# Casting FFN weights in DRAM ahead of their first use, paced by the FFN stages

## The chip, the cores and the metric

The kernel runs on all 8 cores of one Trainium2 chip, two dies of four cores. Each core computes two of the 16 sequences; the cores exchange nothing. The metric is the device time of one execution in microseconds (us): that of the slowest core.

Many executions fall into a slower state, whatever the kernel: all cores of one die, sometimes of both, show a lower granted clock and the time is several per cent longer. Such executions are called slow and are not compared. Fast ones of one kernel lie within about one per cent of each other.

## The reference, cut to what matters

```python
D_MODEL, BATCH, SEQ, D_FF = 1024, 16, 2048, 2816
def reference(x, ...):
    for l in range(2):
        x = ln(alpha*x + 0.5*swiglu(x, ffn_w_gate_up[l,0], ffn_w_down[l,0]))   # FFN 0, FFN 2
        y = hgrn2(x, ...) if l == 0 else forgetting_attention(x, k, v, c, ...)
        x = ln(alpha*x + y)
        x = ln(alpha*x + 0.5*swiglu(x, ffn_w_gate_up[l,1], ffn_w_down[l,1]))   # FFN 1, FFN 3
        if l == 0: k, v, c = shared_kv(x, ...)
    return x
```

The four FFNs carry most of the arithmetic. One has 22 gate/up tiles (1 MB each in float32, 0.5 MB in bf16) and 5.8 MB of down weights in bf16. All inputs are float32; the kernel multiplies in bf16.

## The kernel before

A core walks over 8 blocks of 512 tokens. The work is recorded as a sequence of tokens; `p0` is FFN 0 of the first two blocks together, `a`, `c`, `d`, `e` are FFN 0, 1, 2, 3 of one block, `h` the recurrence, `k` the keys and values, `x` the attention. Recurrence and attention are a second thread, woven into the FFN stages by a list scheduler. That scheduler works at build time, with a cost model, and fixes the order of instructions on each engine.

```python
head = "p0 i2 h0 a2 h1 h2 c0 k0 d0 x0 c1 k1 d1 x1 c2 k2 d2 e0 x2 i3 a3 e1 h3 i4 a4"
```

Weights come through one helper. At the first use GpSimd's DMA queue (POOL) casts float32 in DRAM to bf16 in SBUF, and the plain queue of SyncE (SP) writes the bf16 tile back to a scratch in DRAM; every later use is a plain load from that scratch.

```python
def wload(self, th, key, dst, bufs, chan, scr, src, nb):
    R = self.R
    wb = self.wsb.get(key)
    if wb is None:                                     # first use
        wb = self.wsb[key] = Buf()
        R.dma("pool", [(dst, src)], reads=..., writes=bufs, chan=chan, nbytes=nb)
        R.dma("sp", [(scr, dst)], reads=bufs, writes=[wb], chan=self.wch.next(), nbytes=nb)
    else:
        R.dma("sp", [(dst, scr)], reads=[wb], writes=bufs, chan=chan, nbytes=nb)

def ffn(self, blocks, f):                              # cut
    for half in range(2):
        for jj in range(HJ):                           # 2 x 11 steps
            j = half * HJ + jj
            w = self.wg.next()                         # a ring of 5 tiles
            self.wload(0, ("gu", f, j), w.t[:], ...)
            if jj in (1, 3, 5): ...                    # a group of down weights into wd
            ...                                        # 16 matmuls a block, ACT, DVE -> hT[:, jj]
        ...                                            # down projection, layer norm in the second half
```

The softmax here doesn't subtract the row's maximum and nothing guards it: scores larger than these inputs give would overflow.

## Time and profile before

| | before |
|---|---|
| executions | 5817.2, 5830.1, 5835.0, 5844.3 us; two slow ones 6309.9 and 6460.6 us |
| core 3 of the profile | 5825.7 us, PE busy 94% |

The profile of before caught a slow execution: die 1 ran at a clock of 0.925. So I read core 3, on the undisturbed die. PE is the matrix engine. An FFN stage is taken to end with the last matmul that reads the down weights `wd` (each block has 176 of them, so the count gives the stage). The stages of core 3, in order p0, a2, c0, d0, c1, d1, c2, d2, e0, by the table of stretches; the columns are the stretch, its length, the busy time of PE, weight loads, DVE, ACT and POOL with their instructions, the granted PE clock, the DMA share (mean busy share of 16 DMA engines) and GB/s:

```profile
core 3: us, PE busy (x) PEld busy (x) DVE busy (x) ACT busy (x) POOL busy (x), PEclk, DMA share, GB/s
0.00:331.00 331.00, 279.14 (x1178) 120.44 (x1179) 125.00 (x215) 39.73 (x61) 26.51 (x54) 0.88 0.79 175
331.00:544.00 213.00, 191.59 (x1015) 87.57 (x1013) 138.02 (x297) 108.26 (x235) 19.88 (x25) 0.97 0.73 191
544.00:801.00 257.00, 215.73 (x1111) 98.38 (x1110) 154.96 (x320) 116.64 (x247) 30.93 (x43) 0.92 0.88 214
801.00:1133.00 332.00, 279.06 (x1440) 129.19 (x1438) 201.47 (x398) 136.96 (x271) 33.88 (x53) 0.91 0.90 214
1133.00:1311.00 178.00, 167.27 (x1039) 83.78 (x1038) 92.64 (x158) 58.59 (x114) 5.50 (x10) 0.98 0.67 215
1311.00:1474.00 163.00, 151.64 (x699) 67.16 (x697) 69.15 (x110) 25.98 (x38) 3.23 (x4) 0.97 0.60 182
1474.00:1648.00 174.00, 168.41 (x1044) 84.69 (x1043) 92.96 (x158) 58.82 (x114) 4.39 (x8) 0.98 0.59 196
1648.00:1809.00 161.00, 148.02 (x694) 65.73 (x692) 68.54 (x109) 25.87 (x38) 6.69 (x10) 0.99 0.68 202
1809.00:2046.00 237.00, 194.92 (x1356) 99.16 (x1354) 91.43 (x158) 91.56 (x177) 17.34 (x31) 0.91 0.87 211
```

Length minus PE busy is PE's idle time: 42 us in e0, 41 and 53 us in c0 and d0, 6 to 13 us in each of c1, d1, c2 and d2. The stages with first uses (p0, c0, d0, e0) have a DMA share near 0.8 to 0.9, the others about 0.6 to 0.7.

Names in the views: `wg` is the ring of gate/up tiles, `wd` the down weights, `wgu_s` and `wdn_s` their bf16 scratch in DRAM, `lw` a weight tile of the recurrence or attention, `rD` and `rL` residual rows, `xbD` and `xbL` layer norm's output in bf16, `mv` layer norm's statistics, `hT` the FFN's hidden values, `pb` a PSUM bank.

What e0's PE waited for (waiter, awaited: us in total, times, longest):

```profile
PE pb L1096 <- DMA fka_2_72<-ka_d: 30.7, 3, 22.9
PE pb L1096 <- DMA fka_2_73<-ka_d: 5.4, 1, 5.4
PE pb L686 <- ACT xbD L677: 4.3, 2, 2.7
...
PE pb L639 <- DMA wg_7<-w_gu: 0.4, 1, 0.4
```

The awaited load is not a weight: `fka` holds the attention's keys. It is late because SP's queue is full of e0's write-backs and other traffic, as the issue timeline of SP shows (start, time that the issue took, what):

```profile
1825.83 0.34 SPq L242 DMA_DIRECT2D rD_17<-xr_d  x1
1826.21 3.21 SPq L242 DMA_DIRECT2D rL_21<-xr_d  x1
1832.27 12.05 SPq L242 DMA_DIRECT2D wdn_s<-wd  x2
1844.36 15.00 SPq L242 DMA_DIRECT2D fka_2_72<-ka_d  x1
```

An issue takes about 0.3 us when the queue has room, and 15 us for `fka` here.

### The profile page before, as it was taken

The numbers are of one execution on the slowest core, as the hardware profiler recorded it, in microseconds if no ns is written. First come the engines' busy times: TensorE is split into PE (matmuls) and PEld (weight loads), VectorE is DVE, ScalarE is ACT, GpSimd is POOL, SyncE is SP. The second block draws the span as 40 slices with busy tenths as digits, with TensorE's granted clock in tenths as the row PEclk, the third lists the DMA queues.
The fourth block names the chain that finished last, engine by engine and source line by source line (L and its number), as shares of the span: only waits on it lengthen the run. The fifth ranks groups of instructions, "written<-read, shape, count | busy, mean of one in ns | idle before, by whom it ended". The sixth has DMA issues, their size and how long they took to land.

```text
span 6089.9 us, 77661 instructions; the slowest of 8 cores (5798.2 to 6089.9 us)
## 1 busy us (share of the span) xinstructions
PE 5759.3 (95%) x31296; PEld 2685.6 (44%) x31296; DVE 3064.1 (50%) x5516; ACT 2134.0 (35%) x4154; POOL 272.7 (4%) x410
## 2 busy tenths in 40 slices
PE   6987979999998999999999999999999999999999
PEld 2443434444444444444544454444544444534543
DVE  2466656554542567674557535674245543333344
ACT  0153535322214153442325262442513415514510
POOL 0001111000000000000000000000000000000000
PEclk9998989999998999999999999999888788878887
DMA  9678897775678656566564656555354454454344
GB/s 213 155 201 217 194 240 183 222 222 184 199 185 219 211 188 204 178 196 196 180 211 147 200 182 205 177 189 197 109 192 151 148 169 137 135 181 146 109 157 137
DMA packets 383494, 1106.28 MB, mean 182 GB/s; under 512 B 66784, under 2 KB 80800, under 8 KB 370592
## 3 DMA queue, kind: packets, MB, share of 16 engines
q1 hardware_dynamic: 353840, 1004.80, 50.1%
q0 software_dynamic: 29296, 96.51, 10.1%
q8 instruction: 248, 4.06, 0.3%
q14 instruction: 110, 0.90, 0.1%
HBM read 989.54 MB, written 208.14 MB: 197 GB/s over the span
## 4 chain that ended last, share of the span: by engine, by line
PE 84%; DMA 8%; DVE 3%; ACT 2%; issue 2%; POOL 0%; SPq 0%; POOLq 0%; DVEq 0%
PE pb L639 73%; PE pb L1096 4%; PE pb L1112 2%; DMA wg_6<-w_gu 1%; PE pb L686 1%; PE pb L949 1%; DMA fka_2_72<-ka_d 1%; DMA lw_38<-hqf_s 1%; DMA wg_9<-wgu_s 1%; DMA wg_7<-w_gu 1%; DMA ka_d<-hT 1%; PE pb L928 1%; DMA wgu_s<-wg_7 1%; DMA xr_d<-rL_21 1%; PE pb L945 0%
## 5 line engine op out<-in xcount | busy, mean ns | idle before, releaser
L639 PE MATMUL pb<-wd,hT 128*128 128x512 bf16 x5456 | 1319.6, 396 | 6.3 <-DVE sg_14 L723 3.3
L639 PEld LDWEIGHTS pb<-wd,hT 128*128 128x128 bf16 x5456 | 539.3, 101 | 656.1 <-issue 219.8
L720 ACT ACTIVATE sg_13<-pb 128x512 f32<-128x512 f32 x352 | 209.9, 596 | 977.7 <-PE pb L639 976.2
L720 ACT ACTIVATE sg_14<-pb 128x512 f32<-128x512 f32 x352 | 210.0, 596 | 973.5 <-PE pb L639 971.2
L723 DVE SCALAR_TENSOR_TENSOR sg_14<-sg_14,pb 128x512 f32<-128x512 f32 x352 | 241.5, 686 | 569.4 <-ACT sg_14 L720 568.7
L723 DVE SCALAR_TENSOR_TENSOR sg_13<-sg_13,pb 128x512 f32<-128x512 f32 x352 | 241.5, 686 | 510.3 <-ACT sg_13 L720 509.5
L726 DVE SCALAR_TENSOR_TENSOR hT<-sg_14,pb 128x512 bf16<-128x512 f32 x352 | 241.2, 685 | 201.2 <-PE pb L639 186.9
L726 DVE SCALAR_TENSOR_TENSOR hT<-sg_13,pb 128x512 bf16<-128x512 f32 x330 | 225.9, 685 | 190.1 <-PE pb L639 179.2
L639 PE MATMUL pb<-xT_3,wg_6 128*128 128x512 bf16 x880 | 223.0, 403 | 44.3 <-DMA wg_6<-w_gu 42.7
L639 PE MATMUL pb<-xT_4,wg_10 128*128 128x512 bf16 x912 | 232.9, 405 | 7.7 <-DVE hT L980 5.3
L639 PE MATMUL pb<-xT_3,wg_10 128*128 128x512 bf16 x880 | 218.9, 399 | 18.7 <-DMA wg_10<-w_gu 8.0
L639 PE MATMUL pb<-xT_3,wg_8 128*128 128x512 bf16 x896 | 224.4, 399 | 10.7 <-DMA wg_8<-w_gu 8.7
L639 PE MATMUL pb<-xT_4,wg_6 128*128 128x512 bf16 x912 | 229.7, 403 | 0.0
L639 PE MATMUL pb<-xT_3,wg_7 128*128 128x512 bf16 x880 | 221.4, 401 | 8.3 <-DMA wg_7<-w_gu 6.0
L639 PE MATMUL pb<-xT_4,wg_9 128*128 128x512 bf16 x848 | 216.2, 405 | 7.2 <-ACT hT L977 1.8
L639 PE MATMUL pb<-xT_4,wg_8 128*128 128x512 bf16 x880 | 220.2, 400 | 2.7 <-DVE hT L980 1.0
L639 PE MATMUL pb<-xT_4,wg_7 128*128 128x512 bf16 x864 | 216.3, 400 | 1.3 <-ACT hT L977 0.9
L639 PE MATMUL pb<-xT_3,wg_9 128*128 128x512 bf16 x880 | 214.4, 394 | 0.3 <-DMA wg_9<-wgu_s 0.3
L639 PE MATMUL pb<-xT_5,wg_9 128*128 128x512 bf16 x592 | 144.7, 390 | 12.9 <-DMA wg_9<-wgu_s 9.0
L639 PEld LDWEIGHTS pb<-xT_3,wg_6 128*128 128x128 bf16 x880 | 87.8, 102 | 154.3 <-issue 66.2
L639 PE MATMUL pb<-xT_5,wg_7 128*128 128x512 bf16 x608 | 147.6, 387 | 3.5 <-DVE sg_14 L723 1.9
L1105 ACT ACTIVATE fPT_2_76<-pb 128x512 bf16<-128x512 f32 (+1 forms) x216 | 122.3, 566 | 73.6 <-PE pb L1096 40.2
(507 smaller groups left out, 9471.2 us busy)
## 6 DMA issues: line engine op xcount, KB each, us to landing
wd<-wdn_s SPq DMA_DIRECT2D x108, 1024.0 KB, 7.4
wg_9<-wgu_s SPq DMA_DIRECT2D x120, 512.0 KB, 4.4
wg_10<-wgu_s SPq DMA_DIRECT2D x120, 512.0 KB, 4.6
wg_8<-wgu_s SPq DMA_DIRECT2D x119, 512.0 KB, 4.6
wg_7<-wgu_s SPq DMA_DIRECT2D x118, 512.0 KB, 4.5
wg_6<-wgu_s SPq DMA_DIRECT2D x117, 512.0 KB, 4.6
wd<-wdn_s SPq DMA_DIRECT2D x54, 768.0 KB, 9.6
wd<-w_dn POOLq DMA_DIRECT2D x16, 1024.0 KB, 16.9
```

The costliest lines, as they stand in the source:

```text
L639: ins = e.matmul(out, lhsT=pairs[i][0], rhs=pairs[i][1], start=(start and i == 0), stop=(stop and i == n - 1))
L686: ins = e.transpose(qv[:, k, :], xb.t[:, k * 128:(k + 1) * 128], self.ident.t[:])
L720: R.op("act", lambda e, sg=sg, pg=pg: e.activation(out=sg.t[:], in_=pg.t[:], func=AF.Tanh, scale=0.5), reads=[pg.b], writes=[sg.b], cost=c ...
L723: R.op("dve", lambda e, sg=sg, pg=pg: e.scalar_tensor_tensor(out=sg.t[:], in0=sg.t[:], scalar=1.0, in1=pg.t[:], op0=ALU.add, op1=ALU.mult) ...
L726: R.op("dve", lambda e, sg=sg, pu=pu, jj=jj, hT=hT: e.scalar_tensor_tensor(out=hT[:, jj, :], in0=sg.t[:], scalar=0.25, in1=pu.t[:], op0=AL ...
L928: ins = e.matmul(Uv[:, x, :], lhsT=bt.t[:, t, :], rhs=V.t[:, t, hv], start=True, stop=True)
L949: R.op("pe", lambda e, t=t, cc=cc, c=c, pov=pov, A=A, sp=sp: e.matmul(pov[cc * 64:(cc + 1) * 64, t, :], lhsT=A.t[:, c * 64:(c + 1) * 64], ...
L1096: first = ins = e.matmul(ps.t[:, c0:512], lhsT=ka.t[:, i * 128:(i + 1) * 128], rhs=qa.t[:, h4, c0:512], start=True, stop=(i < 4 * b))
L1105: R.op("act", lambda e, ps=ps, pt=pt, c0=c0: e.activation(out=pt.t[:, c0:512], in_=ps.t[:, c0:512], func=AF.Exp), reads=[ps.b], writes=[pt ...
L1112: ins = e.matmul(accv[:, t, 0:65], lhsT=pt.t[:, t * 128:(t + 1) * 128], rhs=Vt.t[:, i, vo:vo + 65], start=(i == 0 and t == 0), stop=(i == ...
```

## The change

The intent: some weights of FFN 1, 2 and 3 are cast from DRAM to the bf16 scratch in DRAM in an earlier FFN stage, one tile or down group at a time, each released by a step of that stage. Their first use is then a plain load, and the write-back falls away. FFN 1: 17 of 22 gate/up tiles, in the second half of p0 and in a2. FFN 2: 8 tiles, in c0. FFN 3: all 22 tiles and the 6 down groups, in c1, d1, c2, d2. That is 53 casts.

```diff
+    def precast(self, key, gate):
+        if key[0] == "gu":
+            scr, src, nb = self.wgu_s[key[1:]], self.wgu_f[key[1:]], 1 << 19
+        else:
+            ...                                   # the rows of one down group
+        wb = self.wsb[key] = Buf()
+        self.R.dma("pool", [(scr, src)], reads=[gate], writes=[wb], chan=self.cch, nbytes=nb * 1.3)
@@ record
+        gu = lambda f, a, b: [("gu", f, j) for j in range(a, b)]
+        dn = lambda f: [("dn", f, half, g) for half in range(2) for g in range(3)]
+        pre = {"p0": [None] * 11 + gu(1, 0, 11), "a2": gu(1, 11, 17), "c0": gu(2, 0, 8),
+               "c1": gu(3, 0, 7), "d1": gu(3, 7, 14), "c2": gu(3, 14, 22), "d2": dn(3)}
@@ ffn
+        npq = list(self.pq)
+                due = len(npq) * (j + 1) // NJ - len(npq) * j // NJ
+                step = [Buf()] if due else []
-                        reads=[sg.b, pu.b], writes=[hTb[jj]] + ([self.gate] if ...),
+                        reads=[sg.b, pu.b], writes=[hTb[jj]] + step + ([self.gate] if ...),
+                for _ in range(due):
+                    key = self.pq.pop(0)
+                    if key:
+                        self.precast(key, step[0])
```

`chan=self.cch` makes each precast wait for the one before.

## The prediction

> **What bounds the kernel now.** I read core 3, the slowest of the undisturbed die (5825.7 us). By its page the matrix engine (PE) is busy 94% and the chain of waits is 83% PE, 8% DMA: PE-bound, except early. The table of 100 us windows:
> - 0 to 500 us (FFN 0, two blocks at once): 72 us idle, 51 of it in the first 100 us, on first weight loads.
> - 500 to 1150 us (first uses of FFN 1 and 2): about 95 us idle, DMA share 0.77 to 1.01. The PE timeline shows waits for `lw` loads (9.9, 8.6, 14.8 us) and for stores and loads behind `hT`, `xb`, `rD`.
> - 1800 to 2000 us (first use of FFN 3): 42 us idle, DMA share 0.97 and 0.78; waits of 22.9, 6.4, 5.4 us for `fka<-ka_d`. The issue timeline shows single SP issues taking 12 and 15 us: the queue is backed up.
> - 1150 to 1800 us: DMA share 0.5 to 0.7, PE 88 to 100% busy, with room. After 2050 us PE idles about 2%.
>
> **What the change does.** From the packet records, a cast packet leaving 4096 B takes 0.41 us, a plain one 0.20 us. A gate/up tile (128 rows, 16 engines) costs about 3.3 us of all 16 engines to cast, 1.6 us to write back. A whole first-use FFN needs about 160 us (estimate), against 52 us read from scratch. The change drops the write-back but adds a reload, so the total hardly moves; work moves in time. (The Trainium skill, "DMA: Bandwidth & Descriptors", section "Issuing engines are not separate DMA queues", says all issuers share 16 engines, so I count one budget; section "SWDGE vs HWDGE vs iDMA" says a casting DMA must come from GpSimd. The trace agrees: all casts stand on POOL's queue.) Estimates, DMA time:
> - FFN 0, second half: +36 us (11 casts); the next FFN stage +20 us (6).
> - First use of FFN 1: -29 us; of FFN 2: -26 us.
> - c1, d1, c2, d2: +23, +23, +26, +39 us, into a share of 0.5 to 0.7.
> - First use of FFN 3: -110 us.
>
> **Critical path.** At FFN 3 nearly all DMA idle should go: 35 us. In 500 to 1150 us the load falls by a tenth and SP no longer stands behind write-backs of 17 and 8 tiles: 25 to 35 us of 95. Against it, FFN 0's second half (share 0.85) gets more; each precast waits for the one before, on the in-order POOL queue, ahead of FFN 0's own casts (landing in 10 to 24 us): 10 to 20 us lost. The casts in 1150 to 1800 us cost at most 5 us. Steady state is unchanged. Net 40 to 65 us.
>
> **Predicted time:** fast executions lie at 5817 to 5844 us. I expect 5778 us, 8 in 10 between 5715 and 5845. Chances: faster by over 2% 0.13, within 2% 0.82, slower by over 2% 0.05.
>
> **What would show it.** Right: in 1800 to 2000 us PE idle under 15 us, DMA share under 0.75, no long `fka` wait; 53 fewer casts into `wg` and `wd`, as many fewer write-backs; DMA share up by 0.2 in 1200 to 1700 us without new idle; in 500 to 1150 us idle of 60 to 70 us. Wrong: new waits in 200 to 500 us on `wg<-w_gu` or `wg<-wgu_s`.
>
> **What would make it wrong.** DRAM-to-DRAM casts much dearer than casts into SBUF; POOL stuck behind precasts, so that layer norm's `pow` is late; casts that finish after their first use; a shifted order of the list scheduler in the steady state.

## More of the kernel before

The costs of casts at their first use, from the list of DMA issues (destination, source, queue, count, KB, median us from issue to landing):

```profile
wg_6<-w_gu POOLq DMA_DIRECT2D x20, 512.0 KB, 9.3
wgu_s<-wg_6 SPq DMA_DIRECT2D x20, 512.0 KB, 10.9
```

## The result, and the profile after

The kernel after took 5847.29 us in the median of its 10 timed executions, 4 of them slow; the fast ones lie between 5840.7 and 5847.7 us. The ratio to before is 1.0026, 95% interval 1.0010 to 1.0042. Ratios here are the mean time of one kernel's fast executions over that of the other's in the same rounds, so not quite the ratio of the medians. The change is worth nothing, or costs a quarter of a per cent.

The profile of after is a fast one. Core 3 again, by stages:

```profile
core 3: us, PE busy (x) PEld busy (x) DVE busy (x) ACT busy (x) POOL busy (x), PEclk, DMA share, GB/s
0.00:308.00 308.00, 243.56 (x1096) 108.26 (x1097) 110.57 (x192) 31.99 (x50) 28.35 (x58) 0.94 0.90 190
308.00:536.00 228.00, 200.37 (x1029) 90.36 (x1027) 139.93 (x293) 107.87 (x230) 21.57 (x31) 0.95 0.82 200
536.00:802.00 266.00, 231.93 (x1228) 107.91 (x1228) 173.26 (x358) 127.92 (x265) 31.38 (x43) 0.95 0.83 200
802.00:1115.00 313.00, 265.53 (x1376) 122.44 (x1377) 191.69 (x381) 132.61 (x267) 30.36 (x42) 0.92 0.82 205
1115.00:1318.00 203.00, 177.05 (x1051) 87.44 (x1049) 95.66 (x162) 59.57 (x115) 9.84 (x18) 0.92 0.81 222
1318.00:1482.00 164.00, 151.59 (x700) 67.15 (x699) 69.33 (x111) 25.98 (x38) 6.90 (x11) 0.97 0.73 207
1482.00:1669.00 187.00, 170.22 (x1042) 84.59 (x1040) 92.00 (x157) 58.84 (x114) 8.72 (x16) 0.97 0.72 202
1669.00:1836.00 167.00, 152.90 (x698) 67.46 (x697) 69.52 (x110) 25.87 (x38) 6.92 (x10) 0.96 0.82 212
1836.00:2031.00 195.00, 188.97 (x1350) 97.46 (x1348) 92.67 (x160) 90.43 (x177) 4.99 (x9) 0.98 0.61 188
```

e0 (last row) is 42 us shorter, with 6 us idle; its DMA share fell from 0.87 to 0.61. But a2, c0, c1 and c2 (rows 2, 3, 5 and 7) are longer by 15, 9, 25 and 13 us; d0 is 19 us shorter, d2 6 us longer. The first row must be read with care. In before, core 3 ran at a clock of 0.81 for 144 us of p0, and the cores beside it did not:

```profile
100.00:239.00 139.00, 137.75 (x639) 62.29 (x638) 50.76 (x74) 17.32 (x29) 10.23 (x18) 1.00 0.83 166
...
100.00:239.00 139.00, 138.06 (x527) 57.04 (x526) 41.26 (x60) 13.12 (x22) 9.79 (x18) 0.81 0.75 152
```

(cores 1 and 3 of before, the same stretch.) The Trainium skill, "TensorE: Matmul & The Clock Gate", section "Seeing it yourself", describes a peak-current limiter that takes a whole die to 13/16 of the clock. The recorded 0.8125 is that value, but here two cores of die 0 had it and two did not. So p0's 23 us on core 3 are no gain of the change. I ran the kernel before once more for a profile with all cores fast (`before_again` below); its stages are the "before" of what follows.

PE's longest waits in c1 before:

```profile
PE pb L686 <- ACT xbD L677: 3.8, 2, 3.4
PE pb L1096 <- DMA fka_2_72<-ka_d: 3.7, 2, 2.4
```

c1 of the kernel after, and e0:

```profile
PE pb L658 <- DMA wg_8<-wgu_s: 10.8, 1, 10.8
PE pb L1122 <- DMA fka_2_72<-ka_d: 7.4, 2, 4.2
PE pb L705 <- ACT xbD L696: 4.4, 3, 2.7
```
```profile
PE pb L705 <- ACT xbD L696: 4.3, 2, 2.7
...
PE pb L1122 <- DMA fka_2_73<-ka_d: 0.3, 1, 0.3
```

e0's wait for `fka` is gone, as it was meant to be. The stage gains more than that wait: in core means of before_again and after, PE's idle time in e0 fell from 37.6 to 6.0 us and its busy time from 197 to 189 us, and the granted clock stood at 0.5 for 42 us of e0 before and for 5 us after. In c1 there is a new wait on a plain load, of a weight tile from scratch (10.8 us). The wait for `fka` there is longer on this core, but not new: in core means the wait for weights from scratch grew from 3.9 to 11.6 us, that for `fka` from 6.2 to 6.4 us. In p0 and a2, after 200 us, there are new waits too, of 9.7 us for `wg_7<-w_gu` and 6.8 us for `wg_7<-wgu_s`.

The casts themselves are no dearer from DRAM to DRAM:

```profile
wgu_s<-w_gu POOLq DMA_DIRECT2D x47, 512.0 KB, 9.3
...
wdn_s<-w_dn POOLq DMA_DIRECT2D x4, 1024.0 KB, 15.8
```

A packet of 4096 B took 0.39 to 0.44 us, by core (means over c1 to d2), against 0.40 to 0.41 us into SBUF before.

### The profile page after: what moved, and what is told of

It reads as the page before. It is cut to its first block, busy times and chain, and to the rows that moved or that the text cites. A ratio compares the mean times of both kernels' runs of the same rounds, so it can differ in the third digit from the quotient of the medians.

```text
span 5816.4 us, 77659 instructions; the slowest of 8 cores (5778.8 to 5816.4 us)
## 1 busy us (share of the span) xinstructions
PE 5464.8 (94%) x31296; PEld 2602.2 (45%) x31296; DVE 3057.3 (53%) x5516; ACT 2128.1 (37%) x4154; POOL 272.8 (5%) x410
## 3 DMA queue, kind: packets, MB, share of 16 engines
q0 software_dynamic: 29296, 96.51, 10.8%
## 4 chain that ended last, share of the span: by engine, by line
PE 83%; DMA 9%; DVE 4%; ACT 3%; issue 2%; SPq 0%; POOL 0%; DVEq 0%; POOLq 0%
PE pb L658 72%; PE pb L1122 4%; PE pb L1138 2%; DMA ka_d<-hT 1%; DMA wg_8<-wgu_s 1%; PE pb L705 1%; PE pb L975 1%; DMA wg_6<-w_gu 1%; DMA wg_7<-w_gu 1%; PE pb L954 1%; DMA lw_38<-hvg_s 1%; PE pb L971 1%; DMA wg_7<-wgu_s 1%; DMA fka_2_73<-ka_d 0%; PE pb L1125 0%
## 5 line engine op out<-in xcount | busy, mean ns | idle before, releaser
L658 PE MATMUL pb<-wd,hT 128*128 128x512 bf16 x5456 | 1244.0, 379 | 6.9 <-DVE sg_14 L745 4.1
L658 PEld LDWEIGHTS pb<-wd,hT 128*128 128x128 bf16 x5456 | 522.4, 98 | 604.3 <-DVE hT L748 8.1
L658 PE MATMUL pb<-xT_3,wg_6 128*128 128x512 bf16 x880 | 212.4, 389 | 47.0 <-DMA wg_6<-w_gu 43.1
L658 PE MATMUL pb<-xT_3,wg_7 128*128 128x512 bf16 x880 | 209.2, 384 | 14.6 <-DMA wg_7<-w_gu 14.6
L658 PE MATMUL pb<-xT_4,wg_10 128*128 128x512 bf16 x912 | 215.2, 382 | 7.9 <-DVE hT L1006 5.4
L658 PE MATMUL pb<-xT_3,wg_8 128*128 128x512 bf16 x896 | 210.4, 382 | 11.6 <-DMA wg_8<-w_gu 7.4
L658 PE MATMUL pb<-xT_4,wg_8 128*128 128x512 bf16 x880 | 207.2, 381 | 13.0 <-DMA wg_8<-wgu_s 10.8
L658 PE MATMUL pb<-xT_3,wg_10 128*128 128x512 bf16 x880 | 208.4, 384 | 8.6 <-DMA wg_10<-w_gu 8.6
L658 PE MATMUL pb<-xT_4,wg_6 128*128 128x512 bf16 x912 | 213.4, 382 | 0.1
L658 PE MATMUL pb<-xT_3,wg_9 128*128 128x512 bf16 x880 | 204.9, 379 | 0.9 <-DVE sg_13 L745 0.8
L658 PE MATMUL pb<-xT_4,wg_9 128*128 128x512 bf16 x848 | 198.1, 379 | 7.3 <-DVE hT L1006 2.8
L658 PE MATMUL pb<-xT_4,wg_7 128*128 128x512 bf16 x864 | 201.1, 379 | 3.5 <-ACT hT L1003 1.8
L658 PE MATMUL pb<-xT_5,wg_9 128*128 128x512 bf16 x592 | 146.2, 394 | 21.6 <-DMA wg_9<-wgu_s 18.7
L658 PE MATMUL pb<-xT_5,wg_7 128*128 128x512 bf16 x608 | 147.3, 387 | 11.8 <-DMA wg_7<-wgu_s 7.9
```

Source lines behind the costliest of these rows:

```text
L658: ins = e.matmul(out, lhsT=pairs[i][0], rhs=pairs[i][1], start=(start and i == 0), stop=(stop and i == n - 1))
```

## The experiments

All kernels here are the kernel after with the shown edit. Stage times are medians over the cores of a profile, in us; two cores, whose traces lack some matmul records, are left out, and in `only_f12` the slow die. p0 and a2 are added, and c0 and d0, because the scheduler shifts work over the border between them. The last column is the end of e0.

| kernel | casts moved | p0+a2 | c0+d0 | c1 | d1 | c2 | d2 | e0 | end of e0 | ratio to before (95%) |
|---|---|---|---|---|---|---|---|---|---|---|
| before_again | 0 | 521 | 567 | 190 | 162 | 173 | 164 | 233 | 2015 | |
| after | 53 | 526 | 580 | 201 | 163 | 183 | 167 | 195 | 2018 | 1.0026 (1.0010 to 1.0042) |
| only_f3 | 28 | 524 | 566 | 199 | 163 | 186 | 168 | 196 | 2007 | 0.9991 (0.9938 to 1.0045) |
| only_f12 | 25 | 547 | 580 | 188 | 162 | 173 | 164 | 241 | 2062 | 1.0042 (1.0008 to 1.0076) |
| only_f1 | 17 | 532 | 574 | 190 | 162 | 173 | 163 | 237 | 2026 | 1.0030 (0.9991 to 1.0069) |
| tiny (wrong result) | 53, a few rows | 576 | 568 | 193 | 162 | 173 | 163 | 194 | 2029 | |
| twice | 53, doubled | 591 | 601 | 214 | 185 | 212 | 211 | 202 | 2220 | 1.0360 (1.0302 to 1.0418) |
| d_only | 13 | 524 | 574 | 190 | 163 | 172 | 168 | 208 | 1993 | 0.9970 (0.9941 to 1.0000) |
| slots | 28 | 518 | 570 | 189 | 168 | 175 | 171 | 195 | 1987 | 0.9967 (0.9936 to 0.9999) |
| front | 28 | 519 | 572 | 213 | 161 | 182 | 166 | 194 | 2009 | 1.0013 (0.9967 to 1.0059) |
| best | 28 | 524 | 581 | 184 | 167 | 176 | 169 | 195 | 1997 | two fast executions |
| seven_left | 21 | 530 | 568 | 191 | 164 | 174 | 167 | 195 | 1981 | 0.9953 (0.9934 to 0.9971) |
| seven_again | 21 | 524 | 577 | 187 | 163 | 175 | 169 | 195 | 1987 | 0.9937 (0.9882 to 0.9991) |

After e0 all kernels need the same time to the end, within some 20 us. The kernels without casts in p0, a2 and c0 should agree in the first two columns, so their spread (518 to 530, 566 to 581) is the noise of one profile. In c1 to e0 it is a few us.

**only_f3: the half for FFN 3.**

```diff
-        pre = {"p0": ..., "a2": ..., "c0": ..., "c1": gu(3, 0, 7), "d1": gu(3, 7, 14), ...}
+        pre = {"c1": gu(3, 0, 7), "d1": gu(3, 7, 14), "c2": gu(3, 14, 22), "d2": dn(3)}
```

> Only the precasts of FFN 3 are left (28 casts in c1, d1, c2, d2); those of FFN 1 and 2 are gone. Stage times, medians of undisturbed cores, before / after: a2 210/230, c0 252/265, d0 323/314, c1 186/201, d1 161/163, c2 173/183, d2 163/167, e0 234/195 us. Theory A (the traffic of the moved casts slows the loads of the stages that they run in): a2, c0, d0 go back to before's times, e0 stays near 195, but c1 stays near 200 and c2 near 183; sum of a2 to e0 about 10 us under before, ratio to before about 0.998. Theory B (the casts themselves are nearly free; c1 and c2 were lengthened by the changed order of instructions and by backlog left over from the casts for FFN 1 and 2): c1 is back at 186 to 190 and c2 at 173 to 177, e0 near 195, sum about 30 us under before, ratio about 0.995.

e0 falls by 37 us and c1, d1, c2, d2 rise by 9, 1, 13 and 4, together 27 us. The stages before them are as in before. So the lengthening of c1 and c2 is there without the casts for FFN 1 and 2: theory B's backlog is not its cause. What runs in c1 and c2 itself is: the traffic of the casts, or the order of instructions that they bring. The run `tiny` tells these apart.

**only_f12: the other half.**

```diff
+        pre = {"p0": [None] * 11 + gu(1, 0, 11), "a2": gu(1, 11, 17), "c0": gu(2, 0, 8)}
```

> Only the precasts for FFN 1 and 2 (25 casts in p0, a2, c0) are left. Both theories: e0 is again near 234 us with waits for fka loads, a2 stays near 230 and c0 near 265, so this half of the change alone loses: ratio to before 1.001 to 1.006. Theory A: c1 is back near 186, for no cast runs there. Theory B: c1 stays near 200, since its wait comes from the changed order and from the backlog of the stages ahead of it.

As expected, this half alone loses, 0.4%. c1 is back at 188, which again speaks for theory A. The waits for `fka` in e0 are back.

**tiny: the order of the change without its traffic.**

```diff
-        self.R.dma("pool", [(scr, src)], reads=[gate], ...
+        self.R.dma("pool", [(scr[0:16], src[0:16])], reads=[gate, self.fill], ...
+        # at the start of record(): the rest of each scratch filled with 0.01 from SBUF, no cost to the scheduler
```

> The changed kernel in the same order of instructions, but each precast moves 16 of its rows only (an eighth of a gate/up tile, a thirty-second of a down group), so the result is wrong on purpose; the scratch is filled with a constant by DMAs at the very start, which makes p0 about 100 us longer and makes the time useless; stages from a2 on are what is read. Theory A (traffic): a2 falls from 230 to under 215, c1 from 201 to under 190, c2 from 183 to under 176, e0 stays near 195. Theory B (order and queues): they stay within 5 us of the changed kernel's 230, 201 and 183.

The order of instructions is that of the change, but c2, d1 and d2 are back at before's times; c1 is at 193, just over the 190 that I had set, and p0+a2 can't be read because of the filling (a2 alone had 203 us). So the traffic lengthens c1 and c2, and the changed order at most 3 us of c1. `tiny` also frees POOL sooner, so the late `pow` of layer norm, which the prediction names (GpSimd computes it behind the casts on its queue), has to be looked for in the waits: DVE waited 0.8 to 2.1 us a stage for POOL's `mv` in c1 to d2 of the change, and 0.7 to 2.1 us in before_again (core means). It is not the cause there. There is a second reading: c0+d0 is at 568, although here the casts and write-backs of 25 tiles have left these stages, and next to nothing took their place (by the packet records, 56 us of DMA time less). The reference is 567. So taking DMA work out of c0 and d0 did not shorten them. That it could not, is not shown: the order here is that of the change, and a loss by the order may hide a gain. In core means of c0 and d0 together, PE's waits for `lw` and `wg` loads are 21 us in before_again and in `tiny`, while those for `oall` (results of recurrence and attention) and `hB` (of the recurrence) rose from under 1 and 2.2 us to 5.1 and 7.4 us. No run takes the two apart.

**twice: the traffic doubled.**

```diff
-        self.R.dma("pool", [(scr, src)], ...
+        self.R.dma("pool", [(self.wx[0:src.shape[0], 0:src.shape[1]], src), (scr, src)], ...
```

> Every precast is moved twice by one issue (the second copy to a scratch that nobody reads), the order of instructions unchanged: about +23 us of 16 engines' time in each of c1, d1, c2, +39 in d2, +20 in a2, +36 in p0, +26 in c0. Theory A: another +10 to +15 us in c1, +5 to +10 in c2, +10 to +20 in a2, about +60 us in all, ratio to before about 1.012. Theory B: under 20 us in all, ratio to before under 1.006.

Far more than theory A expected: 3.6% in place of 1.2%. From the packet records of c1 to d2 together: with the precasts of the change there are 117 us more of 16 engines' time in these stages (34, 26, 31 and 26 us), and the stages are 25 us longer than in before_again (11, 1, 10, 3). The second copies add another 152 us of DMA time, and the stages grow by another 108 us (13, 22, 29, 44). Per us of DMA time that is 0.2 us first and 0.7 us then. But this is not the price of traffic alone. In d2 of core 3, PE now waits for layer norm's rows and for weights from scratch; DVE waits for POOL, and POOL for its own casts:

```profile
PE pb L658 <- DVE rD L776: 34.6, 1, 34.6
PE pb L658 <- DMA wg<-wgu_s: 17.1, 3, 15.1
DVE rD L683 <- POOL mv L681: 37.0, 2, 36.6
POOL wx L242 <- DMA wdn_s<-w_dn: 133.8, 5, 35.4
```

Here the late `pow` did happen: it stood behind chained casts on POOL's queue. From the change to `twice`, PE's waits in c1 to d2 grew by 94 us (core means), about 44 of them on DMA loads and 43 on `rD`. Without these 43 us the price would be about 0.4 us (an estimate: 108 less 43, over 152). So traffic itself seems to become dearer, but by how much this run does not settle.

**slots and front: the same casts, elsewhere in the same stages.** If it is traffic, what sets its price? Cut into 20 us slices, the packet record shows that the plain queue alone fills the DMA engines for 20 to 40 us at a time, above all at stage borders: layer norm's rows go out, new rows, the three groups of down weights and the keys come in. Between these bursts the share moves between about 0.2 and 0.8. Theory A1: a cast costs where it meets a burst. Theory A2: it costs the same everywhere.

```diff
# slots
+        pre = {"c1": at((6, 8, 9, 15, 17, 19, 20), gu(3, 0, 7)),
+               "d1": at((6, 8, 9, 15, 17, 19, 20), gu(3, 7, 14)),
+               "c2": at((5, 7, 8, 9, 15, 17, 19, 20), gu(3, 14, 22)), "d2": at((5, 8, 10, 15, 18, 20), dn(3))}
# front
+        pre = {"c1": at(range(7), gu(3, 0, 7)), "d1": gu(3, 7, 14),
+               "c2": at(range(8), gu(3, 14, 22)), "d2": dn(3)}
# at(steps, keys): keys[i] is released by step steps[i] of the stage's 22
```

> FFN 3's 28 casts alone, in the same stages, but kept off the steps near stage boundaries and the reload of the down weights, where the record of packets shows the plain queue at a share of 0.9 to 1.0. Theory A1 (bursts): c1 falls from 199 to 187 to 193, c2 from 186 to 174 to 180, e0 stays at 196; a2 to e0 about 1670 us, ratio 0.996. Theory A2 (proportional to DMA time wherever it falls): c1 and c2 stay within 4 us of 199 and 186, ratio 0.999.

> The opposite of the run before: c1's 7 and c2's 8 casts stand in the first steps of their stage, one a step, in the burst of the stage boundary; d1 and d2 as in the change. Theory A1: c1 at 205 us or more and c2 at 192 or more, ratio 1.001 or more. Theory A2: c1 and c2 as in the evenly paced run, 199 and 186.

c1: 213 us with the casts in front, 199 evenly paced, 189 off the bursts, and 190 with no cast. c2: 182, 186, 175 and 173. For c1 theory A1 held as expected. For c2 `slots` did what A1 expected, but `front` was no worse than the even pace, and not the 192 expected. So A2 falls: 7 casts in c1 cost 23 us or nothing, by their place. A1 holds for c1, and in part for c2. d1 and d2 got 5 and 3 us longer than in only_f3 (163 and 168) in `slots`. For d1 the steps that I chose are not the reason: in `best`, below, its casts are evenly paced as in only_f3, and it is at 167 too. Part of what c1 saves may be paid in d1. c1 and d1 together took 352 us with no cast, 362 evenly paced, 374 in `front`, 357 in `slots` and 351 in `best`, so the place still decides.

The start of c1 in `front`, by slices of 20 us (c1 starts at 1069 us):

```profile
1070.00:1090.00 20.00, 13.69 (x68) 6.18 (x67) 12.22 (x18) 4.84 (x6) 1.68 (x3) 0.85 1.01 258
1090.00:1110.00 20.00, 16.46 (x99) 7.81 (x97) 7.40 (x13) 7.13 (x16) 1.09 (x2) 0.98 1.02 290
1110.00:1130.00 20.00, 7.25 (x31) 3.12 (x31) 0.79 (x2) 1.85 (x4) 0.00 (x0) 0.57 0.99 242
1130.00:1150.00 20.00, 19.01 (x133) 9.85 (x131) 7.05 (x15) 8.82 (x20) 1.07 (x2) 1.00 0.78 172
```

and in `slots` (c1 starts at 1104 us):

```profile
1105.00:1125.00 20.00, 13.70 (x69) 6.23 (x68) 12.40 (x18) 4.64 (x6) 1.10 (x2) 0.84 0.97 339
1125.00:1145.00 20.00, 19.49 (x119) 9.54 (x118) 8.09 (x14) 8.14 (x18) 0.00 (x0) 0.98 0.98 327
1145.00:1165.00 20.00, 16.50 (x127) 8.77 (x126) 5.77 (x13) 9.26 (x22) 1.64 (x3) 1.00 0.93 239
1165.00:1185.00 20.00, 20.00 (x154) 10.84 (x152) 6.47 (x14) 10.73 (x25) 0.52 (x1) 1.00 0.74 195
```

Both have a full DMA for 60 us. In `front` the casts take their part of it (the third slice has 0.22 of cast packets and 0.76 of plain ones, 242 GB/s), the plain loads land later, and PE is busy 7 of 20 us. Its clock suffers as well: PE waited from 1107 to 1122.8 us, and the granted clock was 0.5 from 1111.5 to 1128.5 us. In `slots` the plain queue has the engines for itself in the first two slices (327 to 339 GB/s) and PE has no long wait. The wait itself, in `front`'s c1:

```profile
PE pb L662 <- DMA wg<-wgu_s: 15.8, 1, 15.8
PE pb L1126 <- DMA fka<-ka_d: 13.3, 3, 6.9
```

and in `slots`' c1, where no weight is waited for:

```profile
PE pb L1126 <- DMA fka<-ka_d: 4.7, 2, 3.3
PE pb L709 <- ACT xbD L700: 3.8, 2, 3.4
```

A tile's 16 matmuls take about 3.5 us, so a ring of five looks about 17 us ahead. The mean landing time of weight loads from scratch in c1 was 9.6 us in before_again, 10.0 in slots, 12.3 in front and 13.0 in the kernel after; of the slowest tenth in c1 the landing took at least 16.4, 15.9, 23.3 and 25.4 us. The loads in the tail are those that are later than the ring looks ahead.

**d_only: less than half of FFN 3's casts, by number.**

```diff
+        pre = {"d1": gu(3, 0, 7), "d2": dn(3)}
```

> Less than half of FFN 3 is precast: 7 gate/up tiles in d1 and the 6 down groups in d2, nothing in c1 and c2, nothing for FFN 1 and 2. In the run with FFN 3's 28 casts alone, c1 and c2 grew by 13 us each and d1 and d2 by 2 and 5, e0 fell by 38. Theory A1 (bursts: a cast costs where it meets the full plain queue, and c1 and c2 have such bursts, d1 and d2 fewer): c1 186, c2 173, d1 163, d2 168; e0 falls by at least half of 38, to 210 to 215, since its load falls from 0.86 to about 0.75; a2 to e0 about 12 to 18 us under before, ratio 0.996 to 0.998. Theory A2 (cost and gain are both in proportion to DMA time): d1 and d2 cost 14 us together, e0 falls by 20, net 6 us or less, ratio 0.999.

Near to what A1 expected: 13 of 28 casts moved (but over half of the bytes, for the down groups are larger) bring 25 of the 38 us, and cost 5. The DMA share of e0 is still 0.81 here. Its gain does not follow its DMA time either, which fell by 36 of the change's 84 us; it goes with the wait for `fka` (8.4 us on core 3 in place of 36.1).

**only_f1: does c0 gain from being relieved?**

```diff
+        pre = {"p0": [None] * 11 + gu(1, 0, 11), "a2": gu(1, 11, 17)}
```

> Only FFN 1's 17 casts, in p0 and a2. The prediction's sum says that c0, whose own load then falls by about 55 us of DMA time (17 write-backs and 17 casts fewer, 17 reloads more), gains 12 to 17 us. Theory A: a2 is at 226 to 230 as with the whole change; c0 and d0 together, whose boundary shifts with the order of work, fall from 575 by no more than 12 us (the run with tiny casts, with the load taken off both, had 566); net no gain, ratio 1.000 to 1.004. If the prediction's sum is right, c0 and d0 together fall to 550 or below.

By the packet records c0 loses 33 us of DMA time, and not the 55 of the expectation; its share falls to about 0.75. c0+d0 take 574 us, against 567 before and 566 to 581 in kernels that do nothing there. No gain is seen. p0+a2 grow by 11 us. The casts of p0's second half also run into a2: chained, and each landing after 7 to 26 us (core 3 of the kernel after), the last of p0's eleven was issued at 347 us, 39 us after p0's end.

**before_again: before, with all cores fast.**

> The kernel before, unchanged, for a profile with all cores in the fast state: the profile of before had one slow die and two cores with a throttled stretch in p0. Every theory: p0 and a2 together 520 to 535 us, c0 and d0 565 to 580, c1 186, d1 161, c2 173, d2 163, e0 230 to 240.

As expected. It serves as the reference of the table.

**best, seven_left and seven_again: a version that gains.**

```diff
# best: c1 and c2 as in slots, d1 and d2 as in the change
+        pre = {"c1": at((6, 8, 9, 15, 17, 19, 20), gu(3, 0, 7)), "d1": gu(3, 7, 14),
+               "c2": at((5, 7, 8, 9, 15, 17, 19, 20), gu(3, 14, 22)), "d2": dn(3)}
# seven_left and seven_again: no cast in c1; the last 7 tiles of FFN 3 are cast at first use
+        pre = {"d1": gu(3, 0, 7), "c2": at((5, 7, 8, 9, 15, 17, 19, 20), gu(3, 7, 15)), "d2": dn(3)}
```

> FFN 3's 28 casts: in c1 and c2 kept off the bursts, as in the run slots (c1 189, c2 175), in d1 and d2 evenly paced, as in the change (d1 163, d2 168). If stages add up (theory A1): c1 189, d1 163, c2 175, d2 168, e0 195, sum of a2 to e0 about 1668 us against 1702 before, ratio 0.994 to 0.996. If the gain of slots in c1 and c2 was only moved to the stages after it (rival: the DMA work left over has to be paid somewhere), d1 and d2 are at 168 and 171 again and the ratio is 0.997.

> As best, but c1 has no cast, and FFN 3's last 7 gate/up tiles are cast at first use. Theory A1: c1 187, e0 at 195 to 201, because seven casts late in e0 do not meet the loads of fka at the start of the attention; ratio 0.994 to 0.996. If e0's gain goes with its DMA time: e0 falls by 28 of 38 us only, to 206, ratio 0.997.

> The kernel of the run seven_left once more, since six of its eight executions were slow ones: if its ratio of 0.9953 from two fast executions holds, this one is between 0.993 and 0.998, with e0 at 192 to 199 us; if it was luck of two executions, the ratio is 0.998 or more.

`best` is inconclusive: c1 and c2 are as added up, d1 (167) and d2 (169) nearer to the rival's numbers, and c0+d0 is at 581, for which no cause was looked for; only two of its executions were fast. `seven_left` keeps the whole gain of e0 (195 us) with 21 casts, for a few us in d1, c2 and d2, and its two runs have ratios of 0.9953 and 0.9937, both intervals under 1 (from two and three fast executions). By its ratios it beats before by about half a per cent, and the kernel after, at 1.0026, by more. That it is better than `slots` or `d_only` is not shown: the intervals overlap. e0 of seven_again on core 3, its stretch and its longest waits:

```profile
1759.00:1955.00 196.00, 189.12 (x1358) 97.58 (x1356) 93.98 (x161) 90.61 (x177) 8.85 (x16) 0.99 0.72 208
```
```profile
PE pb L709 <- ACT xbD L700: 4.3, 2, 2.7
PE pb L1126 <- DMA fka<-ka_d: 1.3, 2, 0.9
```

## Why the prediction was wrong

The median of 5847.29 us is 2 us above the range; the real error is that a gain of 40 to 65 us was forecast and none came. By its steps:

- **The budget of DMA time: right for c1 to d2, p0 and a2, half right for c0 and d0.** Forecast for c1, d1, c2, d2: +23, +23, +26, +39 us, 111 together; measured 34, 26, 31, 26, together 117. For e0 -110, measured -84 (d2 of before already holds 17 us of packets of e0's casts). For p0 and a2 +56, measured +57, but more of it in a2. For c0 and d0 -55, measured -28 (c0 -1, d0 -27). Up to the end of e0 the total, which was to hardly move, rose by about 60 us, some 20 of them cast packets. DRAM-to-DRAM casts cost 0.39 to 0.44 us a packet, so the first point of "what would make it wrong" did not happen. The prediction drew on the Trainium skill, "DMA: Bandwidth & Descriptors", section "Issuing engines are not separate DMA queues", for one common budget; casts on POOL's queue delayed loads on SP's (in c1 they landed after 13.0 us in the mean, against 9.6 without casts).
- **"At FFN 3 nearly all DMA idle should go: 35 us": right.** 38 us (233 to 195), with the `fka` waits gone. The DMA share there, forecast under 0.75, was 0.61.
- **"The casts in 1150 to 1800 us cost at most 5 us": the failed step.** They cost 27 us in only_f3, and 25 us in the whole change (11, 1, 10, 3). I read a stage's mean DMA share of 0.6 to 0.7 as room. The mean is made of bursts at 1.0 and of quiet stretches; front and slots show that the place decides: 23 us or nothing for the same 7 casts in c1 (with d1 counted in, 22 us or at most 5). What PE then waited for were plain loads that landed late, above all weights from scratch (in c1 3.9 us before, 11.6 in the change, 17.5 in `front`, 3.1 in `slots`, core means). `twice` shows that what room there is ends, partly in DMA time and partly in POOL's queue.
- **"In 500 to 1150 us ... 25 to 35 us of 95": failed too.** In the change c0's load hardly fell, for its own eight precasts took the room of what left it. But c0+d0 did not get shorter in only_f1 (574 against 567), where c0's load fell by 33 us, nor in tiny (568), where 56 us of load left the two stages and next to nothing replaced it. So the step from a tenth less load to 25 to 35 us less idle time failed: a share of 0.9 beside idle time was taken for its cause. What holds c0 and d0 was not settled, and a loss by the changed order is not excluded (see `tiny`); the waits that stay in c0 (core mean of only_f1) are 7 us for layer norm's `xbL`, 5 for `oall`, 3 for `lw`, each short and each behind something else. In the change a new wait of 20 us on core 3 stands in k0, on `vst`, whose buffers (values on their way to DRAM) wait for their stores. It was 20 to 26 us by core with real casts, 3 us in the mean with tiny ones, and none in only_f1, which leaves out c0's eight precasts; so it goes with the traffic of those eight.
- **"10 to 20 us lost" in FFN 0's stages: about right.** 5 us in the change, 11 in only_f1, 26 in only_f12, in noise of about 6; the new waits on `wg<-w_gu` and `wg<-wgu_s` in 200 to 500 us that were named as the sign of it are there.

With the measured terms: +5 (p0, a2), +13 (c0, d0), +25 (c1 to d2), -38 (e0) is +5 us; the ratio says +15 us. The sum had one right gain of 35 us and two wrong terms, by about 20 and by 25 to 48 us.

The rival theory, that the list scheduler's new order was at fault, accounts for at most 3 us of c1 to e0, in c1 (tiny); for c0 and d0 it stays open. A blocked POOL queue is not seen in c1 to d2 of the change; in a2 DVE waited 8.9 us for POOL's `mv` in the mean, where before_again had no such wait, and no run tells what that cost.

## What to carry to other kernels

A DMA share averaged over a stage is not room: cut the stage into slices as short as the prefetch reaches ahead, and put background transfers into the quiet ones, or leave them out. A high share beside idle time is not proof that the transfers cause the idle time; look which load ends the wait, and ask whether it meets the traffic that you take away. Moving less than all can be worth more than moving all: here 21 casts to well-chosen places gave half a per cent, 53 evenly spread ones nothing. And look what else stands in the queue that issues the background work: in `twice` layer norm waited 37 us for a `pow` that stood behind casts.

## What the Trainium skill lacked or had wrong

- "DMA: Bandwidth & Descriptors", section "Issuing engines are not separate DMA queues", says that the transfers interleave, but gives no price for background traffic. Here the first 117 us of extra DMA time in four stages went with 25 us of stage time, the next 152 us with 108, of which some 43 are layer norm's wait for POOL's queue.
- The same section calls the time that a sequencer needs to initiate a DMA "usually small relative to the DMA itself". Behind other issues, single ones on SP took 5.93 and 15.00 us, against 0.32 us with room.
- The same page has no figure for a casting copy from DRAM to DRAM: 0.39 to 0.44 us per packet of 4096 B written, by core, against 0.40 to 0.41 us into SBUF, and 9.3 us from issue to landing for 512 KB.
- "TensorE: Matmul & The Clock Gate", section "Seeing it yourself", says that the limiter takes a whole die to 13/16 of the clock once a third core runs dense matmuls, and advises to budget for that clock. Slow executions here look like that (6720.25 us, with all cores of die 0 at 0.812 to 0.815). But in fast ones all eight cores ran matmuls for 93 to 94% of the time at a mean granted clock of 0.975 to 0.979 in the profile of the kernel after; and in before cores 2 and 3 of die 0 were at 0.81 for at least 139 us while cores 0 and 1 were at 1.00.
